# Gamma by one broadcast, a load in two transfers, and copies on GpSimd, in an RMS norm that writes each row twice

## The chip, the core and the metric

The kernel runs on one core of one Trainium2 chip. The time is device microseconds of one execution of the program. The engines named here are VectorE (DVE), ScalarE (ACT), GpSimd (POOL) and SyncE (SP); TensorE does no work in this kernel. SP and ACT each have a queue from which they issue DMA transfers, and these run on the core's 16 DMA engines.

## The reference

```python
def reference(x, gamma):                 # x: 8 x 512 x 2048 float32, gamma: 2048 float32
    x_rep = np.repeat(x, 2, axis=1)      # each row twice
    rms = np.sqrt((x_rep ** 2).mean(axis=-1, keepdims=True) + 1e-6)
    return (x_rep / rms * gamma[None, None, :]).astype(np.float32)
```

4096 rows of 2048 numbers are read (33.55 MB), each is divided by its root mean square and multiplied by gamma, and each result is written twice (67.11 MB).

## The kernel before

All rows live in one on-chip tile `y` of 128 partitions by 24 slots, a slot being one row of 2048 floats (8 KB). A load (line 50) brings eight rows to every partition: 65,536 contiguous bytes per partition, 8.39 MB in all. A store (line 53) writes eight slots of every partition, which is four rows with their repeats, also 8.39 MB. There are four loads and eight stores, all issued from SP's queue.

The 24 slots are three regions of eight: `first` = 0, `second` = 8, `third` = 16. The function `four(n, constants)` handles two loads and four stores and runs twice. It loads tile n into slots 4 to 11 (the upper half of `first` and the lower half of `second`) and tile n+1 into `third`, and then makes four regions of results:

1. rows 0 to 3 of tile n, into `first`, in two groups of two rows;
2. rows 4 to 7 of tile n, in place in `second`, from the last row to the first;
3. rows 0 to 3 of tile n+1, from `third` into `first`, once the store of step 1 has left;
4. rows 4 to 7 of tile n+1, into `third`.

For each region `squares` lets ACT sum the squares of every row (line 63, one instruction per row) and take the root (line 67). `scale` lets DVE form the reciprocal (line 73) and write the scaled row into an even slot (line 75, one instruction per row, with gamma as a tensor operand `gamma_b`). `repeat` (line 82) copies the even slots into the odd ones: for regions 1 and 2, half on ACT and half on DVE; for regions 3 and 4, on ACT alone. Then the region is stored. In region 2 DVE's part of the copy is the one of rows 0 and 1 (line 102), the rows that are scaled last.

The function `constants`, called between the issues of the first two loads, brings gamma in from ACT's queue: one transfer of the first 2000 numbers, as 16 pieces of 125 (line 121), and three transfers of 16 numbers each (line 127), into slots 0 to 2 of partition 0. GpSimd spreads them over the 128 partitions of `gamma_b` in two broadcasts (lines 131 and 135). DVE sets the tile `eps_t` (line 136), and a first square root on ACT (line 139) has ACT's function table loaded early.

The order on each engine is the program's order (`manual_schedule`); semaphores between the engines follow from the tiles that are read and written.

Of the kernel before, what the change touches and what calls it, by code (L numbers as in the profile page):

```python
# [1 line left out]

# [4 lines left out]


@with_exitstack
def kernel(  # L10
    ctx: ExitStack,
    tc: tile.TileContext,
    x: bass.AP,
    gamma: bass.AP,
    out: bass.AP,
):
    nc = tc.nc
    P = nc.NUM_PARTITIONS
    f32 = mybir.dt.float32
    Act = mybir.ActivationFunctionType  # L20
    Alu = mybir.AluOpType

    B, S, D = x.shape
    Bo, So, Do = out.shape
    R = So // S
    assert R == 2 and D == Do and B == Bo and So == S * R
    eps = 1e-6
    inv_d = 1.0 / float(D)


    K = 4
    N = B * S
    ntiles = N // (P * K)
    assert N % (P * K) == 0 and ntiles == 8
    H = 2
    x_t = x.rearrange("b s d -> (b s) d").rearrange("(n p k) d -> n p k d", p=P, k=H * K)
    out_t = out.rearrange("b s d -> (b s) d").rearrange("(n p h j) d -> n h p (j d)", p=P, h=H, j=K * R)

    singles = ctx.enter_context(tc.tile_pool(name="singles", bufs=1))
    rows = ctx.enter_context(tc.tile_pool(name="rows", bufs=1))  # L40
    junk = ctx.enter_context(tc.tile_pool(name="junk", bufs=1, space=bass.MemoryType.PSUM))
    small = ctx.enter_context(tc.tile_pool(name="small", bufs=4))

    y = rows.tile([P, 3 * K * R, D], f32, name="y")
    first, second, third = 0, K * R, 2 * K * R

    def load(n, at):
        nc.sync.dma_start(out=y[:, at : at + H * K, :], in_=x_t[n])  # L50

    def store(n, h, to):
        nc.sync.dma_start(
            out=out_t[n, h], in_=y[:, to : to + K * R, :].rearrange("p j d -> p (j d)")
        )

    def squares(at, rows):

        n = len(rows)
        ss = small.tile([P, n], f32, name=f"ss{n}")  # L60
        for c, k in enumerate(rows):
            sq = junk.tile([P, D], f32, name="sq")
            nc.scalar.activation(  # L63
                out=sq[:], in_=y[:, at + k, :], func=Act.Square, accum_out=ss[:, c : c + 1]
            )
        rms = small.tile([P, n], f32, name=f"rms{n}")
        nc.scalar.activation(out=rms[:], in_=ss[:], func=Act.Sqrt, scale=inv_d, bias=eps_t[:])  # L67
        return rms

    def scale(at, to, rows, rms):  # L70
        n = len(rows)
        rstd = small.tile([P, n], f32, name=f"rstd{n}")
        nc.vector.reciprocal(out=rstd[:], in_=rms[:])  # L73
        for c, k in enumerate(rows):
            nc.vector.scalar_tensor_tensor(  # L75
                out=y[:, to + R * k, :], in0=y[:, at + k, :], scalar=rstd[:, c : c + 1],
                in1=gamma_b[:], op0=Alu.mult, op1=Alu.mult,
            )

    def repeat(to, k0, k1, copy):  # L80
        y_r = y[:, to + R * k0 : to + R * k1, :].rearrange("p (k r) d -> p k r d", r=R)
        copy(out=y_r[:, :, 1, :], in_=y_r[:, :, 0, :])  # L82

    ctx.enter_context(tc.manual_schedule())

    half = K // 2
    up, down = list(range(K)), list(range(K - 1, -1, -1))

    def four(n, constants):


        load(n, first + K)
        constants()
        load(n + 1, third)
        for rows in (up[:half], up[half:]):
            scale(first + K, first, rows, squares(first + K, rows))
        repeat(first, 0, half, nc.scalar.copy)
        repeat(first, half, K, nc.vector.tensor_copy)
        store(n, 0, first)
        scale(second, second, down, squares(second, down))  # L100
        repeat(second, half, K, nc.scalar.copy)
        repeat(second, 0, half, nc.vector.tensor_copy)
        store(n, 1, second)
        roots = [squares(third + h * K, up) for h in range(H)]
        scale(third, first, up, roots[0])
        repeat(first, 0, half, nc.scalar.copy)
        repeat(first, half, K, nc.scalar.copy)
        store(n + 1, 0, first)
        scale(third + K, third, up, roots[1])
        repeat(third, 0, K, nc.scalar.copy)  # L110
        store(n + 1, 1, third)

    gamma_b = singles.tile([P, D], f32, name="gamma_b")
    G, E = 16, 3
    C = D // G - E
    gamma_s = y[0:1, 0:2, :].rearrange("p k (c d) -> p (k c) d", c=G // 2)
    gamma_t = y[0:1, 2, :]
    eps_t = singles.tile([P, 1], f32, name="eps_t")

    def constants():  # L120
        nc.scalar.dma_start(
            out=gamma_s[0:1, :, :C],
            in_=gamma[: G * C].rearrange("(p c d) -> p c d", p=1, c=G),
        )
        for c in range(E):
            at = G * C + c * G
            nc.scalar.dma_start(
                out=gamma_t[0:1, c * G : (c + 1) * G],
                in_=gamma[at : at + G].partition_broadcast(1),
            )  # L130
        nc.gpsimd.partition_broadcast(  # L131
            out_ap=gamma_b[:, : G * C].rearrange("p (c d) -> p c d", c=G),
            in_ap=gamma_s[0:1, :, :C],
        )
        nc.gpsimd.partition_broadcast(out_ap=gamma_b[:, G * C :], in_ap=gamma_t[0:1, : E * G])  # L135
        nc.vector.memset(eps_t, eps)  # L136

        root = singles.tile([P, 1], f32, name="root")[:]
        nc.scalar.activation(out=root, in_=eps_t[:], func=Act.Sqrt)  # L139

    four(0, constants)
    four(2, lambda: None)


# [1 line left out]
_INS = ['x', 'gamma']  # L146
_OUTS = [((8, 1024, 2048), 'float32')]


# [23 lines left out]
```

## Time and profile before

| | us |
|---|---|
| median of 3 runs | 238.84 (238.44 to 238.92) |
| the profiled execution's own time | 238.52 |
| its span, first to last instruction | 236.3 |
| busy: DVE, ACT, GpSimd | 84.4, 110.2, 2.8 |
| 16 DMA engines, SP's queue | 98.7% of the span |
| scaling of one row on DVE, 128x2048 | 2.348 |
| copy of 128x4096 on ACT; on DVE | 3.599; 2.294 |
| broadcast of 2000 columns; of 48, GpSimd | 2.243; 0.323 |

How to read what follows: times are in us from the start of the span, except where ns is given. A line of instructions shows the start, the length, the engine, the source line, the operation, output and input, their shapes, and in brackets how long the engine had been idle and what ended the wait. "SPq" is SP's DMA queue, and the time beside it is that of the issue, not of the transfer. In a line of windows the DMA share is the mean busy share of the 16 DMA engines, and a packet's bytes are counted at its start. One packet here is one partition's 65,536 bytes.

### The profile page before, as it was taken

How to read it: one execution, taken by the hardware profiler on the slowest of the kernel's cores; microseconds unless marked ns; L12 is line 12 of the kernel's file. 1: busy time of each engine (PE TensorE's matmuls, PEld its weight loads, DVE VectorE, ACT ScalarE, POOL GpSimd, SP SyncE). 2: the span in 40 equal slices, each digit the busy share in tenths (PEclk: the TensorE clock that was granted, in tenths of full speed). 3: DMA queues.
4: the chain of work that ended last, by engine and by line, in shares of the span. 5: the costliest groups of instructions: out<-in, count | busy, mean ns of one | idle time of the engine just before them, and what ended most of it. 6: DMA issues, size and time to landing. Idle time of an engine off the chain costs nothing.

```text
span 236.3 us, 225 instructions
## 1 busy us (share of the span) xinstructions
DVE 84.4 (36%) x47; ACT 110.2 (47%) x86; POOL 2.8 (1%) x6
## 2 busy tenths in 40 slices
DVE  0000396594699500000000007929919992000000
ACT  2001989479998470000000049991999957400000
POOL 0110000000000000000000000000000000000000
DMA  9898989989898989999898988989898988989894
GB/s 355 356 532 355 521 366 466 422 388 499 355 532 356 521 366 466 422 399 488 355 532 355 510 377 377 510 355 532 355 532 355 510 377 388 499 355 532 355 532 177
DMA packets 1767, 100.68 MB, mean 426 GB/s; under 512 B 230, under 2 KB 230, under 8 KB 230
## 3 DMA queue, kind: packets, MB, share of 16 engines
q1 hardware_dynamic: 1728, 100.66, 98.7%
q10 hardware_dynamic: 38, 0.01, 0.0%
q14 instruction: 1, 0.01, 0.0%
HBM read 33.56 MB, written 67.11 MB: 426 GB/s over the span
## 4 chain that ended last, share of the span: by engine, by line
DMA 45%; ACT 26%; DVE 12%; issue 2%; DVEq 0%
DMA y<-in_x_dram 26%; DMA out_dram<-y 19%; ACT sq L63 15%; DVE y L75 12%; ACT y L82 11%; ACT rms L67 1%; DVE rstd L73 0%; DVEq L75 0%
## 5 line engine op out<-in xcount | busy, mean ns | idle before, releaser
L63 ACT ACTIVATE sq<-y 128x2048 f32<-128x2048 f32 x32 | 60.1, 1878 | 71.1 <-DMA y<-in_x_dram 70.4
L75 DVE SCALAR_TENSOR_TENSOR y<-y,rstd,gamma_b 128x2048 f32<-128x2048 f32 x32 | 73.8, 2348 | 1.6 <-DMA out_dram<-y 1.0
L82 ACT COPY y<-y 128x4096 f32<-128x4096 f32 (+1 forms) x10 | 42.6, 4283 | 19.1 <-DVE y L75 18.3
L73 DVE RECIPROCAL rstd<-rms 128x4 f32<-128x4 f32 (+1 forms) x10 | 1.7, 170 | 109.2 <-ACT rms L67 109.2
L82 DVE COPY y<-y 128x4096 f32<-128x4096 f32 x4 | 9.2, 2294 | 0.1
L63 ACT ACTIVATION_READ_ACCUMULATOR sq<-y 128x1 f32 x32 | 6.0, 186 | 0.0
L67 ACT ACTIVATE rms<-ss,eps_t 128x4 f32<-128x4 f32 (+1 forms) x10 | 3.0, 297 | 0.3
L139 ACT ACT_TABLE_LOAD x1 | 1.3, 1283 | 2.6 <-issue 2.6
L131 POOL PARTITION_BROADCAST gamma_b<-y x1 | 2.2, 2243 | 10.2 <-DMA y<-in_gamma_dram 10.2
L135 POOL PARTITION_BROADCAST gamma_b<-y x1 | 0.3, 323 | 10.2 <-DMA y<-in_gamma_dram 10.2
L136 DVE MEMSET eps_t<- 128x1 f32 x1 | 0.1, 59 | 0.8 <-PEq L157 0.8
L139 ACT ACTIVATE root<-eps_t 128x1 f32<-128x1 f32 x1 | 0.2, 202 | 0.0
L157 POOL MEMSET const-bfloat16-1.0<- 128x1 bf16 x1 | 0.1, 101 | 0.0
L157 POOL MEMSET const-uint8-127<- 128x1 uint8 x1 | 0.1, 101 | 0.0
L157 POOL MEMSET const-float32-0.0<- 128x1 f32 x1 | 0.1, 98 | 0.2 <-issue 0.2
L157 POOL MEMSET const-float32-1.0<- 128x1 f32 x1 | 0.1, 99 | 0.0
## 6 DMA issues: line engine op xcount, KB each, us to landing
out_dram<-y SPq DMA_DIRECT2D x8, 24.7
y<-in_x_dram SPq DMA_DIRECT2D x4, 31.4
y<-in_gamma_dram ACTq DMA_DIRECT2D x3, 0.1 KB
y<-in_gamma_dram ACTq DMA_DIRECT2D x1, 7.8 KB, 9.9
```

Source lines behind the costliest of these rows:

```text
L63: nc.scalar.activation(out=sq[:], in_=y[:, at + k, :], func=Act.Square, accum_out=ss[:, c : c + 1])
L67: nc.scalar.activation(out=rms[:], in_=ss[:], func=Act.Sqrt, scale=inv_d, bias=eps_t[:])
L73: nc.vector.reciprocal(out=rstd[:], in_=rms[:])
L75: nc.vector.scalar_tensor_tensor(out=y[:, to + R * k, :], in0=y[:, at + k, :], scalar=rstd[:, c : c + 1], in1=gamma_b[:], op0=Alu.mult, op ...
L82: copy(out=y_r[:, :, 1, :], in_=y_r[:, :, 0, :])
L131: nc.gpsimd.partition_broadcast(out_ap=gamma_b[:, : G * C].rearrange("p (c d) -> p c d", c=G), in_ap=gamma_s[0:1, :, :C],)
L135: nc.gpsimd.partition_broadcast(out_ap=gamma_b[:, G * C :], in_ap=gamma_t[0:1, : E * G])
L136: nc.vector.memset(eps_t, eps)
L139: nc.scalar.activation(out=root, in_=eps_t[:], func=Act.Sqrt)
L157: nc = _bacc.Bacc("TRN2", target_bir_lowering=False, num_devices=1)
```

## The change

Four things change.

- Gamma goes straight into partition 0 of `gamma_b`, in three transfers from ACT's queue, of 48, 40 and 40 columns in each of 16 pieces. One GpSimd broadcast then spreads that row over all partitions.
- The second load of the first call of `four` is issued as two transfers, partitions 0 to 63 and 64 to 127. The three other loads stay whole.
- `eps_t` is set by GpSimd instead of DVE, ahead of the broadcast.
- In region 2 of each call, the copy of rows 0 and 1 is on GpSimd instead of DVE.

```diff
-    def load(n, at):
-        nc.sync.dma_start(out=y[:, at : at + H * K, :], in_=x_t[n])
+    def load(n, at, parts=(0, P)):
+        for p0, p1 in zip(parts, parts[1:]):
+            nc.sync.dma_start(out=y[p0:p1, at : at + H * K, :], in_=x_t[n, p0:p1])
...
-    def four(n, constants):
+    def four(n, constants, ahead=(0, P)):
         load(n, first + K)
         constants()
-        load(n + 1, third)
+        load(n + 1, third, ahead)
...
-        repeat(second, 0, half, nc.vector.tensor_copy)
+        repeat(second, 0, half, nc.gpsimd.tensor_copy)
         store(n, 1, second)
...
-    G, E = 16, 3
-    C = D // G - E
-    gamma_s = y[0:1, 0:2, :].rearrange("p k (c d) -> p (k c) d", c=G // 2)
-    gamma_t = y[0:1, 2, :]
...
     def constants():
-        nc.scalar.dma_start(
-            out=gamma_s[0:1, :, :C],
-            in_=gamma[: G * C].rearrange("(p c d) -> p c d", p=1, c=G),
-        )
-        for c in range(E):
-            at = G * C + c * G
-            nc.scalar.dma_start(
-                out=gamma_t[0:1, c * G : (c + 1) * G],
-                in_=gamma[at : at + G].partition_broadcast(1),
-            )
-        nc.gpsimd.partition_broadcast(
-            out_ap=gamma_b[:, : G * C].rearrange("p (c d) -> p c d", c=G),
-            in_ap=gamma_s[0:1, :, :C],
-        )
-        nc.gpsimd.partition_broadcast(out_ap=gamma_b[:, G * C :], in_ap=gamma_t[0:1, : E * G])
-        nc.vector.memset(eps_t, eps)
+        nc.gpsimd.memset(eps_t, eps)
+        G = 16
+        g_in = gamma.rearrange("(p c d) -> p c d", p=1, c=G)
+        g_to = gamma_b[0:1, :].rearrange("p (c d) -> p c d", c=G)
+        for c0, c1 in ((0, 48), (48, 88), (88, D // G)):
+            nc.scalar.dma_start(out=g_to[:, :, c0:c1], in_=g_in[:, :, c0:c1])
+        nc.gpsimd.partition_broadcast(out_ap=gamma_b[:], in_ap=gamma_b[0:1, :])
...
-    four(0, constants)
+    four(0, constants, ahead=(0, P // 2, P))
     four(2, lambda: None)
```

More of the change, by code (lines that the diff above doesn't have):

```diff
@@ L113 @@
     gamma_b = singles.tile([P, D], f32, name="gamma_b")
-    G, E = 16, 3
-    C = D // G - E
-    gamma_s = y[0:1, 0:2, :].rearrange("p k (c d) -> p (k c) d", c=G // 2)
-    gamma_t = y[0:1, 2, :]
     eps_t = singles.tile([P, 1], f32, name="eps_t")
     def constants():
-        nc.scalar.dma_start(
-            out=gamma_s[0:1, :, :C],
-            in_=gamma[: G * C].rearrange("(p c d) -> p c d", p=1, c=G),
-        )
-        for c in range(E):
-            at = G * C + c * G
-            nc.scalar.dma_start(
-                out=gamma_t[0:1, c * G : (c + 1) * G],
-                in_=gamma[at : at + G].partition_broadcast(1),
-            )
-        nc.gpsimd.partition_broadcast(
-            out_ap=gamma_b[:, : G * C].rearrange("p (c d) -> p c d", c=G),
-            in_ap=gamma_s[0:1, :, :C],
-        )
-        nc.gpsimd.partition_broadcast(out_ap=gamma_b[:, G * C :], in_ap=gamma_t[0:1, : E * G])
-        nc.vector.memset(eps_t, eps)
-        root = singles.tile([P, 1], f32, name="root")[:]
-        nc.scalar.activation(out=root, in_=eps_t[:], func=Act.Sqrt)
-    four(0, constants)
+        nc.gpsimd.memset(eps_t, eps)
[5 more added lines that the diff above has]
+        nc.gpsimd.partition_broadcast(out_ap=gamma_b[:], in_ap=gamma_b[0:1, :])
+        root = singles.tile([P, 1], f32, name="root")
+        nc.scalar.activation(out=root[:], in_=eps_t[:], func=Act.Sqrt)
+    four(0, constants, ahead=(0, P // 2, P))
     four(2, lambda: None)
```

## The prediction

> **What bounds the kernel now.** I read the page first: engine busy times, the row of DMA by slices, and the queues.
>
> ```profile
> DVE 84.4 (36%) x47; ACT 110.2 (47%) x86; POOL 2.8 (1%) x6
> ...
> DMA  9898989989898989999898988989898988989894
> ...
> q1 hardware_dynamic: 1728, 100.66, 98.7%
> q10 hardware_dynamic: 38, 0.01, 0.0%
> ```
>
> No engine works half of the span, while SP's queue (q1) keeps the 16 DMA engines busy for 98.7% of it. Anything that DVE, ACT or GpSimd does is therefore free as long as the next transfer is issued before the one ahead of it has drained, and anything that makes a transfer itself longer is paid in full.
>
> Second, the windows, cut at the borders between transfers (columns: stretch and length, busy time of DVE, ACT and POOL, clock, DMA share, GB/s).
>
> ```profile
> 0.00:1.50 1.50, 0.06 (x1) 0.00 (x0) 0.19 (x4) 1.00 0.00 0
> 1.50:21.60 20.10, 0.00 (x0) 1.49 (x2) 2.24 (x1) 1.00 1.00 418
> 21.60:40.95 19.35, 11.85 (x7) 17.31 (x16) 0.32 (x1) 1.00 1.00 434
> 40.95:60.28 19.33, 11.70 (x6) 14.28 (x13) 0.00 (x0) 1.00 1.00 434
> 60.28:79.60 19.32, 18.23 (x10) 15.74 (x14) 0.00 (x0) 1.00 1.00 435
> ...
> 215.25:234.60 19.35, 0.00 (x0) 0.00 (x0) 0.00 (x0) 1.00 1.00 434
> ```
>
> In order: start-up, first load, second load, first store, second store, and the last store. Each of the twelve transfers moves 8.39 MB in 19.3 to 20.1 us, loads and stores at one rate, and they stand end to end. Twelve times 19.35 is 232.2 of the 236.3 us span. The packets are 65,536 bytes, eight for each DMA engine in one transfer, so one packet takes 19.35 / 8 = 2.42 us.
>
> Third, the timeline, for how early a store is issued.
>
> ```profile
> 36.88 2.29 DVE L82 COPY y<-y 128x4096 f32<-128x4096 f32 x1
> 39.24 0.35 SPq L53 DMA_DIRECT2D out_dram<-y  x1
> ...
> 53.56 2.29 DVE L82 COPY y<-y 128x4096 f32<-128x4096 f32 x1
> ...
> 55.94 0.34 SPq L53 DMA_DIRECT2D out_dram<-y  x1
> ...
> 60.88 0.18 DVE L73 RECIPROCAL rstd<-rms 128x4 f32<-128x4 f32 x1 [5.03 <-ACT rms L67]
> ```
>
> The first load was issued at 0.72, and finer windows at the start show where its first packets begin:
>
> ```profile
> 1.25:1.50 0.25, 0.00 (x0) 0.00 (x0) 0.00 (x0) 1.00 0.00 0
> 1.50:1.75 0.25, 0.00 (x0) 0.00 (x0) 0.00 (x0) 1.00 1.50 524
> 1.75:2.00 0.25, 0.00 (x0) 0.00 (x0) 0.00 (x0) 1.00 7.24 2359
> ```
>
> Nearly all of them start around 1.75, so an issue needs 1.0 us of lead. The first store must thus be issued by 40.95 - 1.0 = 39.9; it is, at 39.24, with 0.7 to spare. The second store must be issued by 60.28 - 1.0 = 59.3; it is, at 55.94. The second store of the second half of the program is issued at 171.91, and its data is due at 176.65, so by 175.6.
>
> **The second load in two halves (decides).** Removed: one transfer of 128 partitions, 65,536 bytes each. Added: two of 64 partitions with the same 65,536 bytes each, one after the other on SP's queue, so each DMA engine gets four packets of each half, eight in all, as before. The added issue on SP (0.34 us, as the store rows) and its completion lie under the first load, which runs to 21.60. The question is only the rate while a half is moving. No row of before has a transfer of 64 partitions. Lower bound: a packet still takes 2.42 us, because the limit sits in the DMA engine; then the two halves take 2 x 4 x 2.42 = 19.35 and the cost is 0. Upper bound: time goes by what each partition receives, not by how many partitions there are; the nearest rows are the whole loads, with the same bytes per partition, at 19.35 each; two of them take 38.7, and the cost is +19.35. Loads and stores run at the same 434 GB/s, so the limit is on something that both directions pass, the DMA engines or the on-chip memory's side, and hardly in DRAM. The trace doesn't separate these two: each engine always had its own eight partitions. I take the upper end, since the transfer of before most like a half in what a partition gets is the whole load, and because with half of the partitions addressed at any one time, sixteen engines must share paths that serve eight of them now.
>
> [...]
>
> What comes late then: the second load's data lands near 61 instead of 42, and ACT's squares of tile `third` begin near 61 instead of 52.4. Both its stores still have cover, because the first two stores shift too: store one runs 60.3 to 79.6, store two to 98.9. DVE can write `first` again at about 80.8 (it waited for store one at 61.48 before, plus 19.35). From there two scalings (4.7), two more (4.7) and one ACT copy (3.6) put store three's issue near 94, before 97.9. Its successor needs 9.3 of DVE and 7.0 of ACT more, near 110, due at 117. So nothing is added to the 19.35 and nothing is given back: the whole remainder shifts.
>
> **Gamma.** Removed: a transfer of 16 x 500 bytes, three of 64 bytes, and two broadcasts (2243 and 323 ns). Added: three transfers of 16 pieces (192, 160, 160 bytes) and one broadcast of 2048 columns. Broadcast: (2243 - 323) / (2000 - 48) = 0.98 ns per column, so 2.29 us. Landing: in before the first is in at 10.67, where GpSimd's wait ends, and the last at 23.07, so the three small ones took 12.4 / 3 = 4.1 each. They take turns with the load's packets; two turns are 4.84. With 4.84 for each further transfer the third lands at 10.67 + 9.7 = 20.4 and gamma is ready at 22.7; with 4.1 at 21.2; if each took 9.9 like the first, 0.72 + 29.7 + 2.3 = 32.7. DVE's first scaling starts at 27.38, so I count 0, with 4.7 us of cover; the bad end would put the first store 5.3 later, at 44.6, which the long second load (to 60.3) covers. If the halves ran at full rate it would cost 4.6. The DMA engines' own time for three small pieces each is under 0.1 us.
>
> **The memset of eps.** On DVE it took 59 ns at 0.79. GpSimd's own memsets take 101 ns at 0.24 to 0.33; it has nothing else to do, and the ACT instruction that waits for it comes after ACT's four, now three, gamma issues and the 1.28 us table load that ends at 3.87. Cost 0; between -0.1 and +0.1.
>
> **The copy on GpSimd.** Twice per run 128x4096 moves from DVE (2.29 us) to GpSimd. It becomes the last work before the second store, at 53.55 and 169.54; nothing follows it on GpSimd, and behind SP's wait for it stand only later stores. GpSimd has no copy in before. Lower bound 2.29, DVE's; nearest row, the broadcast: 0.28 + 4096 x 0.98 ns = 4.3; upper, if every column is both read and written at that rate, 0.28 + 2 x 4.03 = 8.3. Cover: 59.3 - 53.55 = 5.7 at the first, 175.6 - 169.54 = 6.1 at the second. I take 4.3, the same engine's row: cost 0. With 8.3 the second adds 2.2 and the first, when the load is at full rate, 2.6. DVE gains nothing from the 2.29 us it is rid of: it then idles 5.03 us until ACT's root (row 60.88).
>
> **Sum.** Made against the profiled execution: 238.52 us, 2.2 more than its 236.3 span, and 0.32 under the median 238.84. 238.52 + 19.35 + under 0.1 + 0 + 0 + 0 = 257.9; with the median as base 258.2. I say 258.0.
>
> **Rivals.**
> - *The halves run at the full rate* (not slower): the 2.42 us of a packet belong to the DMA engine. For it: the packets' time is one constant in both directions. Against it: that constant is as well explained by the partitions' side. It decides if a packet of a half takes 2.42 us. Then 238.5 to 238.9, no change. Chance 0.22.
> - *Full rate, but a bubble*: GpSimd's copy takes over 5.7 us, or gamma comes after 28.1. Up to 2.6 + 2.2 = 4.8: 239 to 243.5. Chance 0.06.
> - *The engines slip apart*: where two share a path, one may go first and be in the second half while the other is in the first. Half of the price, +9.7: 248.2. Nothing in before shows an uneven share; all engines' packets take turns. Chance 0.06.
> - *Faster*: the first load moves at 418 instead of 434, (16 / 434) x 20.1 = 0.74 us lost at the start. If four ACT transfers were its cause and three spare all of it, 237.8. The decisive point is 0.48 us saved, the 0.2% that a measurement of this kernel can tell from no change. Chance 0.04.
> - *My forecast*, full price: 0.62. Its own range is 257.5 to 260.5 (GpSimd's 2.2 at the top).
>
> **Numbers.** Slower 0.62 + 0.06 + 0.06 = 0.74; same 0.22; faster 0.04. Full price alone leaves 0.38 out, so the range must reach down to no change: 238.3 to 260.5.
>
> **What would show it.** Right: windows after 21.6 near 217 GB/s until about 60, then 434 again; packets of the second load near 4.84 us; a first store that is issued near 39.3 but waits some 20 us in the queue; squares of `third` that wait for a DMA from about 52 to 61. GpSimd: one broadcast that ends before 27, copies near 4.3 us. Wrong: 434 GB/s right through, with the first store's data at 40.95; or a gap in the DMA row after 60 or 176, which would be GpSimd's copy.

## The result, and the profile after

| | us |
|---|---|
| before, median | 238.64 (238.44 to 238.92) |
| after, median | 259.55 (259.40 to 259.89) |
| ratio | 1.0879, 95% interval 1.0862 to 1.0897 |
| profiled execution after: own time, span | 259.65, 257.5 |

The change makes the kernel 8.8% slower, 20.9 us (the median of before is now that of four runs). The forecast was 258.0, in a range of 238.3 to 260.5.

The first place to look is again the page. These are its engine row, the row of DMA by slices, the GB/s under it, and the queues.

```profile
DVE 79.8 (31%) x44; ACT 110.5 (43%) x86; POOL 9.8 (4%) x8
...
DMA  8979987794997997997998998998998998998994
GB/s 326 490 326 326 316 173 163 163 326 163 489 479 336 489 479 336 489 468 346 489 468 346 489 438 377 489 439 377 489 438 377 489 438 377 489 438 377 489 438 214
...
q1 hardware_dynamic: 1744, 100.66, 98.7%
```

The DMA engines are still busy for 98.7% of a span that is 21.2 us longer, with the same 100.66 MB. So they didn't wait; they moved the same bytes more slowly. The GB/s show where: slices 6 to 8 and 10, between 32 and 64 us, have 163 to 173, and no other whole slice is below 316. (Bytes count at a packet's start, so single slices of the long load, 5 and 9, look better than they are.) The busy share doesn't tell the fast transfer from the slow one: in the windows of the second load it is 1.00 before and 1.01 here. The bytes beside it do, with 434 and 211 GB/s.

The windows, cut at the borders of the transfers (stretch and length, busy time of DVE, ACT and POOL, clock, DMA share, GB/s): first load, second load, first and second store.

```profile
1.50:21.70 20.20, 0.00 (x0) 1.49 (x2) 1.27 (x1) 1.00 0.99 416
21.70:62.00 40.30, 21.26 (x12) 23.91 (x21) 4.62 (x2) 1.00 1.01 211
62.00:81.40 19.40, 0.18 (x1) 16.50 (x18) 0.00 (x0) 1.00 1.00 429
81.40:100.70 19.30, 17.90 (x9) 7.21 (x2) 0.00 (x0) 1.00 1.00 435
```

The second load takes 40.30 us instead of 19.35, which is +20.95. It begins 0.1 later than before, and behind it everything has its old length. That is 21.05 of the 21.2 us. Windows of single rounds, in which each of the 16 engines begins one packet of 65,536 bytes, show the packet's time: two in the first half, the one at the border of the halves, and one in the second.

```profile
26.00:31.20 5.20, 3.41 (x3) 5.14 (x6) 0.00 (x0) 1.00 0.99 202
31.20:36.30 5.10, 5.03 (x4) 4.35 (x5) 0.00 (x0) 1.00 1.01 206
...
41.50:46.40 4.90, 1.79 (x2) 2.98 (x5) 0.00 (x0) 1.00 1.00 214
...
46.30:51.50 5.20, 5.17 (x3) 2.06 (x1) 0.00 (x0) 1.00 0.99 202
```

Within a half a packet takes about 5.13 us (5.11 to 5.14 by the trace's records of the packets), where it was 2.42: somewhat more than double. The round at the border takes 4.90, and the first round, too, is shorter, so the whole load takes 40.30 and not 8 x 5.13 = 41.0.

The timeline shows what the other parts of the change did.

```profile
0.71 0.10 POOL L118 MEMSET eps_t<- 128x1 f32 x1 [0.29 <-POOLq L145]
...
20.43 2.29 POOL L124 PARTITION_BROADCAST gamma_b<-gamma_b  x1 [19.62 <-DMA gamma_b<-in_gamma_dram]
...
54.19 3.60 POOL L83 COPY y<-y 128x4096 f32<-128x4096 f32 x1 [31.46 <-DVE y L76]
57.81 0.34 SPq L54 DMA_DIRECT2D out_dram<-y  x1
63.43 1.88 ACT L64 ACTIVATE sq<-y 128x2048 f32<-128x2048 f32 x1 [10.39 <-DMA y<-in_x_dram]
```

Gamma is ready at 22.7, before DVE's first scaling. GpSimd's copy ends at 57.8, and the second store is issued at once, over 20 us before its turn comes near 81. ACT, which had its next rows at hand before, now waits 10.39 us for the second load.

### The profile page after: what moved, and what is told of

It reads as the page before. It is cut to its first block, busy times and chain, and to the rows that moved or that the text cites. A ratio compares the mean times of both kernels' runs of the same rounds, so it can differ in the third digit from the quotient of the medians.

```text
span 257.5 us, 227 instructions
## 1 busy us (share of the span) xinstructions
DVE 79.8 (31%) x44; ACT 110.5 (43%) x86; POOL 9.8 (4%) x8
## 3 DMA queue, kind: packets, MB, share of 16 engines
q1 hardware_dynamic: 1744, 100.66, 98.7%
## 4 chain that ended last, share of the span: by engine, by line
DMA 59%; DVE 14%; ACT 13%; issue 1%; DVEq 0%
DMA out_dram<-y 35%; DMA y<-in_x_dram 24%; DVE y L76 14%; ACT y L83 7%; ACT sq L64 6%; ACT rms L68 0%; DVE rstd L74 0%; DVEq L76 0%
## 5 line engine op out<-in xcount | busy, mean ns | idle before, releaser
L83 POOL COPY y<-y 128x4096 f32<-128x4096 f32 x2 | 7.2, 3600 | 164.5 <-DVE y L76 164.5
L83 DVE COPY y<-y 128x4096 f32<-128x4096 f32 x2 | 4.6, 2293 | 0.1
L124 POOL PARTITION_BROADCAST gamma_b<-gamma_b x1 | 2.3, 2294 | 19.6 <-DMA gamma_b<-in_gamma_dram 19.6
```

The lines of the kernel that those rows point to most:

```text
L124: nc.gpsimd.partition_broadcast(out_ap=gamma_b[:], in_ap=gamma_b[0:1, :])
```

## The experiments

Three questions were open after the result: whether all of the loss belongs to the split load; if so, whether it comes from there being two transfers, from there being fewer partitions in each, or from which partitions these are; and whether the reckoning of what is hidden holds. "Round" below means one packet on each of the 16 DMA engines.

"Theory P" and its "paths" in the expectations are the author's supposition: that a DMA engine reaches the on-chip memory by a path, that one engine fills a path, and that a group of partitions can have fewer paths than all 128. No trace shows a path. Their numbers are estimates from the rates: in a whole load one engine draws 27.1 GB/s (65,536 bytes in 2.42 us), so the 434 GB/s of before make 16, and the 211 of the split load about eight. What the runs show is the rate of each group of partitions.

### The split alone

```diff
-        nc.sync.dma_start(out=y[:, at : at + H * K, :], in_=x_t[n])      # kernel before
+        for p0, p1 in zip(parts, parts[1:]):
+            nc.sync.dma_start(out=y[p0:p1, at : at + H * K, :], in_=x_t[n, p0:p1])
...
-    four(0, constants)
+    four(0, constants, ahead=(0, P // 2, P))
```

> The kernel before with one edit: the second load is issued as partitions 0 to 63 and then 64 to 127. Theory P (paths): partitions 0 to 63 reach half of the paths into the on-chip memory, so two DMA engines share one path and a packet takes more than twice 2.42 us; the whole 20.9 us of the change come from here: 259.3 to 259.8, packets of the second load at 5.1 us, everything after them at 2.42. Rival G: part of the loss comes from gamma, the memset or the GpSimd copies: this kernel then lies below 259.

Measured: 259.40 us (259.09 to 259.53), ratio 1.0865 [1.0849, 1.0881]. Its second load, by the same kind of window:

```profile
21.70:62.10 40.40, 23.55 (x13) 23.91 (x21) 0.32 (x1) 1.00 1.01 211
```

The split alone has the loss: +20.8 against its own runs of before, where the change has +20.9.

### Everything but the split

```diff
-    four(0, constants, ahead=(0, P // 2, P))      # changed kernel
+    four(0, constants)
```

> The changed kernel with its second load whole again: gamma by one broadcast, eps and the copies on GpSimd stay. Theory P: nothing of these is on the path, 238.4 to 239.0, ratio 0.999 to 1.002. Rival G: they cost something too, over 239.1; the GpSimd copy, 3.6 us in the profile after, would have to end past the time when the second store must be issued (5.7 us after its start), which it does not.

Measured: 238.56 us median, ratio 1.0014 [0.9996, 1.0032]. The median is that of before. The range is wider, though: 238.41 to 240.11 over 12 runs, four of them at 239.9 to 240.1. That called for two more runs, below. The rival by which three gamma transfers shorten the start falls here as well; the first load moves at the same 418 GB/s as before:

```profile
1.50:21.60 20.10, 0.00 (x0) 1.49 (x2) 1.11 (x1) 1.00 1.00 418
21.60:40.95 19.35, 11.85 (x7) 17.35 (x16) 1.18 (x1) 1.00 1.00 434
```

### Two transfers of all 128 partitions

```diff
-        load(n + 1, third, ahead)      # as above, second load whole
+        if n == 0:
+            for c in range(H):
+                nc.sync.dma_start(out=y[:, third + c * K : third + (c + 1) * K, :],
+                                  in_=x_t[n + 1, :, c * K : (c + 1) * K])
+        else:
+            load(n + 1, third)
```

> As no_split, but the second load is in two transfers of 128 partitions with four rows each (32,768 bytes per partition). Theory P: all 16 paths stay in use, so 238.4 to 239.1. Rival S (seams): what costs is that a load is cut in two, with one more transfer, completion and landing; then this is 10 to 21 us slower as well.

Measured: 238.66 us, ratio 1.0007 [0.9996, 1.0018], 238.48 to 239.00 but for one of the ten runs, at 240.03. That a load is cut in two costs nothing that can be measured. Theory S falls.

### The 64 partitions in the middle

```diff
-    four(0, constants, ahead=(0, P // 2, P))      # changed kernel
+    four(0, constants, ahead=((32, 96), (0, 32), (96, 128)))   # pairs, one transfer each
```

> The changed kernel, but the second load is in three transfers: partitions 32 to 95 (64 of them), then 0 to 31, then 96 to 127. [...] Load 4 x 2.42 + 4 x 5.13 = 30.2 instead of 19.35, so 238.6 + 10.8 = 249.4. Rival N (number): the rate goes by the number of partitions in a transfer; the middle 64 are as slow as any 64, packets 5.1 us, and with the groups of 32 slower still: 259.5 or more. Rival S (seams): three transfers cost more than two.

Measured: 248.91 us (two runs, 248.73 and 249.09), ratio 1.0427 [1.0381, 1.0473]. The windows are partitions 32 to 95, then the two groups of 32, then the first store:

```profile
21.60:31.30 9.70, 3.95 (x3) 8.34 (x10) 1.28 (x1) 1.00 1.00 432
31.30:51.00 19.70, 14.70 (x9) 13.97 (x12) 0.00 (x0) 1.00 1.02 216
51.00:70.40 19.40, 2.79 (x3) 18.10 (x19) 3.60 (x1) 1.00 1.01 432
```

This decides between the theories. 64 partitions move at the full 432 GB/s if they are 32 to 95, and at 202 to 206 in the rounds of 0 to 63 and of 64 to 127. It is not the number but which ones. The 4 x 2.42 of the sum was a supposition about 32 to 95 that no run before had shown; the run has 9.70 us for them. The two groups of 32 took 19.70 where the sum has 20.5. The total was forecast within 0.5 us.

No run moved the same partitions to and from other places in DRAM, so a limit by DRAM addresses is spoken against only by argument. The data of the middle 64 partitions lie as close together in DRAM as those of a half, and in the split store below a partition's data lie twice as far apart (131,072 bytes instead of 65,536), with the same rate.

### Four transfers of 32 partitions

```diff
+    four(0, constants, ahead=(0, 32, 64, 96, P))      # changed kernel, P // 2 replaced
```

> The changed kernel, but the second load is in four transfers of 32 partitions. Theory P: 32 partitions reach the same eight paths as 64 do, so the packets stay at 5.1 us and the time at 259.5 (259 to 260.5). Rival N: half the partitions, half the rate again: packets near 10 us, the load near 80 us, 300 us in all. Rival S: two more seams, some 20 us more.

Measured: 259.72 us (259.70 and 259.74), ratio 1.0880 [1.0836, 1.0924], the second load 40.50 us:

```profile
21.60:62.10 40.50, 21.26 (x12) 23.91 (x21) 4.65 (x2) 1.00 1.01 210
```

Half the partitions per transfer at the same rate, 210 GB/s against 211 for the halves, as theory P has it. Theory N falls a second time, and S as well.

### Eight transfers of 16 partitions

```diff
+    four(0, constants, ahead=range(0, P + 1, 16))      # changed kernel, P // 2 replaced
```

> The changed kernel, but the second load is in eight transfers of 16 partitions. [...] Rival N2: a group's rate has nothing to do with how many engines meet; as with 64 and 32 partitions a packet takes 5.12 us and the time is 259.7.

Measured: 293.20 us (292.69 and 293.70), ratio 1.2293 [1.2242, 1.2344]. The windows are one round, and the stretch in which the 16 packets of a later one begin:

```profile
29.80:39.05 9.25, 9.14 (x6) 8.44 (x9) 0.00 (x0) 1.00 1.00 113
48.30:50.50 2.20, 2.17 (x2) 0.21 (x1) 0.00 (x0) 1.00 4.23 477
```

N2 is out by far: a round takes 9.25 us and not 5.12. That is 1.8 times the 5.13 of the halves, and the 113 GB/s are 4.2 times the 27.1 that one engine draws in a whole load. But the second window shows why that is not the rate of 16 partitions alone: the engines begin a round up to 2.2 us apart, and for that time two groups, so 32 partitions, are in use at once. Whether the 6% by which a packet of the halves exceeds the double grows in smaller groups is not shown by this run.

### The same cut in a store

```diff
+        parts = (0, P // 2, P) if n == h == 0 else (0, P)      # loads whole
+        for p0, p1 in zip(parts, parts[1:]):
+            nc.sync.dma_start(out=out_t[n, h, p0:p1],
+                              in_=y[p0:p1, to : to + K * R, :].rearrange("p j d -> p (j d)"))
```

> As no_split, but the first store, not the second load, is in halves of partitions 0 to 63 and 64 to 127. Theory P for both directions: reading from the on-chip memory goes through paths of the same kind, so the packets of the first store take about 5.1 us and the time is 259.5. Rival D (direction): only writes into the on-chip memory are bound by the paths; 238.4 to 239.1.

Measured: 262.46 us (261.92 and 263.00), ratio 1.0995 [1.0925, 1.1064]. A stretch within the second half, the stretch in which the engines begin their first packets behind the cut store, and DVE's wait for that store:

```profile
61.90:77.40 15.50, 0.00 (x0) 7.12 (x9) 0.00 (x0) 1.00 1.01 203
77.50:82.40 4.90, 0.00 (x0) 0.00 (x0) 0.00 (x0) 1.00 0.57 214
```

```profile
84.84 9.14 DVE L79 SCALAR_TENSOR_TENSOR y<-y,rstd,gamma_b 128x2048 f32<-128x2048 f32 x4 [23.80 <-DMA out_dram<-y]
```

The halves have the same rate when they are read from the on-chip memory, 203 GB/s against 202 to 206 in the load, and rival D falls. A store in halves costs 3 us more than a load in halves. The trace shows where: the engines fall out of step. Behind the cut store their 16 first packets begin over 4.9 us, where before a round begins within 0.7, and by the landing records the 16 engines finish the store between 77.9 and 84.7 us (60.7 to 61.4 before; 62.6 to 63.3 for the split load). Their mean is 20.1 us later than before (21.5 for the split load); the last is 23.4 later, and DVE can write `first` at 84.84 instead of 61.48. So it is the slowest engine, and not a slower store as a whole, that costs the 3 us. Why the engines fall out of step in the store and not in the load stays open.

### Both halves at the same time

```diff
-            nc.sync.dma_start(out=y[p0:p1, ...      # changed kernel
+            (nc.scalar if p0 else nc.sync).dma_start(out=y[p0:p1, ...
```

> The changed kernel, but the second half of the second load (partitions 64 to 127) is issued from ACT's queue, behind gamma, so that every DMA engine takes turns between a packet of the first half and one of the second. Theory P with all engines in step: the packets still meet two to a path, 5.1 us each, 259.5. Rival T (turns): where the engines fall out of step, one works on the first half while its fellow is in the second, packets come down towards 2.42, and the time lies between 239 and 255.

Measured: 258.83 us (258.67 and 259.00), ratio 1.0843 [1.0796, 1.0889]. Three rounds:

```profile
26.00:31.12 5.12, 0.00 (x0) 2.46 (x3) 0.00 (x0) 1.00 1.00 205
31.12:35.95 4.83, 2.80 (x3) 4.77 (x6) 0.00 (x0) 1.00 1.01 217
35.95:40.85 4.90, 4.83 (x4) 4.16 (x4) 0.00 (x0) 1.00 1.00 214
```

Two queues save 0.7 us of 20.9. Where the rounds of the two halves alternate they take 4.83 to 4.90 instead of 5.13, so the loss beyond the exact double goes, as in the one border round of the changed kernel (4.90), but the double stays. The engines keep in step: the 16 packets that begin between 31.0 and 32.8 are all of SP's queue, those between 35.9 and 37.6 all of ACT's, and those between 40.8 and 42.5 all of SP's again. Rival T is refuted in its range of 239 to 255.

### How much of GpSimd's copy is hidden

```diff
-        repeat(second, half, K, nc.scalar.copy)      # kernel before
-        repeat(second, 0, half, nc.vector.tensor_copy)
+        repeat(second, 0, K, nc.gpsimd.tensor_copy)
```

> The kernel before, but GpSimd makes all copies of region 2 (ACT's half too), 128x8192 in one instruction. At the profile's 3.60 us for 4096 columns it takes 7.1 us. My reckoning of the cover (5.7 us at the first, 6.1 at the second): the second store is issued at 53.55 + 7.1 = 60.7 instead of by 59.3, +1.4, and its fellow in the second half of the program adds 1.0; 241.0 in all, with a hole of the DMA engines near 60 and near 178. Rival: the lead of 1.0 us that I count for an issue is not needed while the queue still has packets, or later work takes the shift up; then 238.6 to 239.6.

Measured: 241.03 us (240.93 to 241.13), ratio 1.0098 [1.0085, 1.0111]. The timeline and a window at the hole:

```profile
53.51 7.01 POOL L82 COPY y<-y 128x8192 f32<-128x8192 f32 x1 [30.37 <-issue]
...
60.55 0.34 SPq L53 DMA_DIRECT2D out_dram<-y  x1
```

```profile
57.75:60.25 2.50, 0.00 (x0) 2.44 (x5) 2.50 (x1) 1.00 0.97 419
60.25:61.25 1.00, 0.00 (x0) 0.27 (x1) 0.27 (x1) 1.00 0.01 0
61.25:63.75 2.50, 1.90 (x1) 0.00 (x0) 0.00 (x0) 1.00 0.98 419
```

In the middle window no engine begins a packet of data, where before a round began at 60.3. The cover is real, and it ends about where it was reckoned; 241.0 was expected. That the total fits to 0.1 us is in part luck: the round behind the first hole begins at 61.4 instead of 60.3, some 1.1 us late and not 1.4, as its first packets follow the issue by 0.8 us and not by the 1.0 that was counted.

### Gamma alone, and GpSimd's copy alone

```diff
-        repeat(second, 0, half, nc.gpsimd.tensor_copy)      # first kernel: no split, copies on DVE
+        repeat(second, 0, half, nc.vector.tensor_copy)
...
-        repeat(second, 0, half, nc.vector.tensor_copy)      # second kernel: before, this line alone
+        repeat(second, 0, half, nc.gpsimd.tensor_copy)
```

> The kernel before with gamma by one broadcast from three transfers and eps set by GpSimd; loads whole, all of DVE's copies on DVE. In the runs of no_split, 4 of 12 were 239.9 to 240.1, the other eight 238.4 to 238.6; the kernel before had none above 239.3 in 23. Theory G1: the new transfers of gamma bring these runs about, now and then the first store comes too late (it has 0.7 us to spare): here too about a third at 240, median 238.5. Theory C: it is the GpSimd copy; then all runs here lie at 238.4 to 239.0. Theory X: chance, nothing in either.

> The kernel before with nothing changed but the copy of rows 0 and 1 of region 2 on GpSimd. At 3.60 us it ends 2.1 us before the second store must be issued, so all at 238.4 to 239.0 by theories G1 and X. Theory C: about a third of the runs at 239.9 to 240.1, the copy being late in some executions.

Measured: gamma alone 238.59 us, ratio 0.9996 [0.9987, 1.0005], 11 of 12 runs at 238.5 to 238.9 and one at 240.18; the copy alone 238.47, ratio 0.9995 [0.9987, 1.0004], 237.98 to 238.99. So neither costs anything at the median, theory C is out, and the runs near 240 are not a third here. The profile of the gamma kernel is that of the execution of 240.18, and it shows where its time went. The windows are those in which a round begins at the switch from stores to loads: first in the kernel before, then in this one, and in this one the time at which the fifth store was due.

```profile
121.00:121.60 0.60, 0.00 (x0) 0.00 (x0) 0.00 (x0) 1.00 4.03 1748
```

```profile
121.00:121.60 0.60, 0.00 (x0) 0.00 (x0) 0.00 (x0) 1.00 3.03 1311
121.60:123.00 1.40, 0.00 (x0) 0.00 (x0) 0.00 (x0) 1.00 0.33 140
...
157.40:158.05 0.65, 0.00 (x0) 0.62 (x3) 0.00 (x0) 1.00 0.01 0
```

In before all 16 engines begin that round within 0.6 us. Here 12 do, three follow by 123.0, and the last begins at 123.5. So some engines have fallen behind, one by 2 us, and the third load then lands at 140.8 instead of 138.8. The fifth store, which needs its data, is issued at 157.25 instead of 155.26, and near 158 no engine begins a packet. Gamma has been in place for 96 us by the switch, and the first store was issued in time, at 39.43. G1's mechanism is thus not what this execution shows.

Taken together, the runs near 240 are six of 34 in the three kernels that have the new gamma and eps and all 128 partitions in every load and store (four of 12, one of 10, one of 12), and none of 55 in before (44, on two chips) and with the copy alone (11). That speaks against chance and for gamma or eps making such runs more frequent; how, when the loss comes 96 us after gamma is in place, stays open. It is 1.5 us in some executions, and no part of the 20.9.

## Why the prediction was right

**What bounds the kernel.** Right. The DMA engines were read as the only bound, and each part of the change was priced by what it does to them. What stayed under them cost nothing (238.56 us without the split), and two stores issued 1.4 and 1.0 us too late by the reckoning cost 2.4 us in all.

**The halves.** Right in the place and the direction, with the term a little small. The step took the upper bound, that time goes by what each partition receives, at twice 19.35. Measured is 40.30, as a packet within a half takes 5.13 and not 4.84, with shorter rounds at the borders; the term is +20.95 instead of +19.35. This 1.6 is the difference between the 257.9 of the sum and the 259.5 measured. The upper bound was no true bound, because a packet within a half took some 6% beyond the double, the load 4%. As a rule, though, "by what each partition receives" is wrong: the middle 64 partitions had the same bytes each and took half of that. The reason given beside it, that sixteen engines must share the paths of eight when half of the partitions are addressed, was a supposition that the trace of before did not show. The runs agree with it for these two halves, at 202 to 206 GB/s, but not for any half: 32 to 95 had 432. For these two halves both reasons give the same double; that the first did no harm is luck.

**What comes late then.** Right: nothing was added behind the load and nothing given back. ACT's squares begin at 63.43 (61 expected), DVE's write into `first` waits for the first store until 82.73 (80.8), and the third store is issued at 95.53 (94), before its turn at about 99.7. The differences, 1.5 to 2.4 us, are in the main the 1.6 us again.

**Gamma.** Right: the broadcast begins at 20.43 (20.4) and takes 2.29. That a small transfer takes two turns with the large packets, and so 4.84 us, was the better of the two readings: the packets of the second and third transfer begin 4.84 us apart, at 12.05 and 16.89. 4.1, from the mean of the three small ones, would have been too early.

**The memset, the copy.** Both cost nothing, as expected (238.56 us with both and no split). The copy takes 3.60 us where I took 4.3 from the broadcast, so the broadcast's time per column was a poor stand-in; it is as long as the same copy on ACT (3.599). This changed only how much cover was left, 2.1 instead of 1.4.

**The rivals.** The full rate in halves (0.22) is refuted by the kernel with the split alone. A bubble by GpSimd's copy needs a longer copy: twice its work made one. In the split load the engines do not slip apart (they finish within 0.7 us), not even from two queues; in the split store they did, by up to 6.8 us, and it cost time instead of saving half the price. The start is not shortened by one gamma transfer less: 418 GB/s in the first load with three and with four. The chance of 0.62 for the full price was rather low, as the trace could not tell the memory's side from the DMA engine's; one experiment with 64 partitions was needed for that.

## What to carry to other kernels

Where the DMA engines bound a kernel as they do here, cut a transfer along the bytes of each partition and not by partitions 0 to 63 and 64 to 127: the first cost nothing here (238.66 us), the second doubled the transfer's time, for a load (40.30 us instead of 19.35) and for a store (203 GB/s instead of 434). If fewer than all partitions have to move, a load of 32 to 95 went at the full rate, 432 GB/s; a store of them was not run. And read GB/s beside the DMA share; the share alone was 98.7% in both kernels.

## What the runs showed of the hardware that was not expected

- A load of 64 partitions can have the rate of 128: 432 GB/s for 32 to 95, against 211 for 0 to 63 followed by 64 to 127.
- With partitions 0 to 63 or 64 to 127 a packet took 5.13 us, 6% beyond 2 x 2.42, and groups of 32 in a row had the rate of these halves, 210 GB/s against 211. With 16 in a row a round took 9.25, a little under 4 x 2.42 = 9.68, with engines up to 2.2 us out of step.
- A split store cost 23.9 us, a split load 20.9: the engines finished the store up to 6.8 us apart, the load within 0.7, and the slowest one counts.
- GpSimd copies 128x4096 of float32 in 3.60 us and 128x8192 in 7.01, the times of ACT (3.599 and 7.018).
